# Attention scores from fp16 parts: two full products a head against one full and one 64-row product

## The chip, the cores and the metric

The kernel runs on one core of one Trainium2 chip. The metric is the device time of one execution in microseconds, lower is better; before the change it is 3462.16 us, the median of three runs (3456.29 to 3462.77). TensorE multiplies, VectorE, ScalarE and GpSimd (POOL) work elementwise, SyncE (SP) issues most of the transfers.

## What is computed

Two transformer-like blocks run on a sequence of 2048 positions and width 1024, in float32. The change lies in the attention of the second block: four heads of difference attention (two softmaxes each, the second subtracted) and four heads of stick-breaking attention, all with 64 channels a product. Cut to that:

```python
def diff_attention(q, k, v, lam, lam_init, g):        # q, k: (B,S,H,2,64), v: (B,S,H,128)
    s = einsum('bqhrd,bkhrd->bhrqk', qb, kb) * 64 ** -0.5     # per block of 128 queries, causal prefix
    p = softmax(where(mask, s, -inf))
    attn = p[:, :, 0] - lam * p[:, :, 1]
    o = einsum('bhqk,bkhe->bqhe', attn, vb)           # then a headwise RMSNorm

def stick_breaking_attention(q, k, v, g):             # q, k, v: (B,S,H,64)
    z = einsum('bqhd,bkhd->bhqk', qb, kb) * 64 ** -0.5
    log_1mb = where(mask, log_sigmoid(-z), 0)
    suffix = cumsum(log_1mb, reverse=True) - log_1mb
    a = where(mask, exp(log_sigmoid(z) + suffix), 0)
    o = einsum('bhqk,bkhd->bqhd', a, vb)              # then a headwise RMSNorm
```

TensorE is fed fp16. To keep float32 accuracy every operand x is split into a high part (x rounded to fp16) and a low part (what is left, in fp16), and products of the parts are summed in PSUM.

## The kernel before

`block1` is the first block (about 0 to 950 us of the profile), `block2` the attention of the second (about 960 to 1970), then come `out2` and the feed-forward part `ffn`, which no line of the change touches.

`block2` works through six units, in the order stick, diff, diff, stick, diff, diff. A unit has two heads, r = 0 and 1, of 64 channels each: two heads of stick-breaking attention, or the two softmaxes of one difference head. Each unit first gets its q, k and v by projections, `unit_gemm`: for each of four blocks b of 512 positions, `gemm(b)` runs three projections (`gemm_ct`, lines 142 to 144: 24 products of 512 columns each, into a PSUM bank of the pool `pg`, which has two) for k, v and q, and evacuates each: ScalarE writes the high part, VectorE the low part. v goes by transposing transfers to its tile. For k and q, transfers on SP's queue put the parts where the score products want them.

Where they are wanted: k's tile of a head holds its high part on partitions 0 to 63 and its low part on 64 to 127. q's tile holds, for a head, the high part twice (on both halves of the partitions) and the low part twice. One product of 128 rows thus gives high q times (high k + low k), a second low q times (high k + low k). These are lines 831 and 832 of `scores`; a third product on line 834 adds the mask where the stretch of keys reaches the diagonal. A stretch has up to 512 keys; each score tile takes one PSUM bank of the pool `sc`, which has four.

The tiles of k, v and q come from the pool `up` (U), whose slots are 4 KB a partition: k0, k1, two v, four q, 8 a unit, out of UN = 11.

A row is a block of 128 queries, i = 0 to 15, with W = (i + 1) x 128 keys. In `diff`, head 0's score tiles are evacuated by VectorE (line 894, with a running minimum), then ScalarE takes its exponentials (line 899, pieces of up to 1024 keys), then head 1's the same way; line 914 combines both heads. In `stick`, for each head, all score tiles of the row are made; then, piece by piece of 1024 keys from the last to the first, ScalarE takes sigmoids (972), VectorE scans (974) and GpSimd takes differences (980); line 967 is a GpSimd memset that starts a scan. Both then split the weights into high and low parts (`parts`, lines 844 and 845), turn them by a transposing transfer on SP (847), and multiply them with v (`spread`, lines 868 and 869). The pieces lie in tiles of the pool E, of which there are EN = 10.

The order of each engine's instructions is fixed when the program is built, by a planner that follows the program on a clock of its own: an engine takes the earliest instruction of the program whose operands and buffers are ready. So the projections of the next unit, which stand later in the program, are spread into the gaps of the current one. A tile gets its slot when the first instruction that writes it is placed.

Of the kernel before, what the change touches and what calls it, by code (L numbers as in the profile page):

```python
# [7 lines left out]
F32 = mybir.dt.float32  # L8
# [9 lines left out]
S = 2048  # L18
# [23 lines left out]
UN = 11  # L42
# [24 lines left out]
class Kernel:  # L67
# [713 lines left out]
    def unit_gemm(self, cols):  # L781


        nc = self.nc
        wk, wq, wv = [self.weight(self.a["w2"][cols[c]]) for c in (1, 0, 2)]
        ks = [self.up.tile([128, S], F16, tag="u", name=f"k{r}") for r in range(2)]
        vs = [self.up.tile([128, NT // 2, 2, 128], F16, tag="u", name="v") for _ in range(2)]
        qs = []

        def gemm(b):  # L790
            bs = slice(b * 512, (b + 1) * 512)
            ps = self.gemm_ct(wk, b)
            kh = self.one.tile([128, 512], F16, tag="kh", name="kh")
            kl = self.one.tile([128, 512], F16, tag="kl", name="kl")
            nc.scalar.copy(kh, ps)
            nc.vector.tensor_tensor(kl, ps, kh, ALU.subtract)
            for r in range(2):
                rs = slice(r * 64, (r + 1) * 64)
                nc.sync.dma_start(ks[r][0:64, bs], kh[rs])
                nc.sync.dma_start(ks[r][64:128, bs], kl[rs])  # L800
            ps = self.gemm_ct(wv, b)
            vt = self.one.tile([128, 2, 512], F16, tag="vt", name="vt")
            nc.scalar.copy(vt[:, 0], ps)
            nc.vector.tensor_tensor(vt[:, 1], ps, vt[:, 0], ALU.subtract)
# [12 lines left out]
        return (qs, ks, vs), gemm  # L817

    def scores(self, ops, r, i, strict):

        nc = self.nc
        qs, ks, _ = ops
        q = qs[i // 4][:, r, :, i % 4 * 128:(i % 4 + 1) * 128]
        W = (i + 1) * 128
        out = []
        for p in range(0, W, 512):
            n = min(512, W - p)
            ps = self.score_tile()
            kk = ks[r][:, p:p + n]
            last = p + n == W  # L830
            nc.tensor.matmul(ps[:, 0:n], q[:, 0], kk, start=True, stop=False)  # L831
            nc.tensor.matmul(ps[:, 0:n], q[:, 1], kk, start=False, stop=not last)  # L832
            if last:
                nc.tensor.matmul(
                    ps[:, n - 128:n], self.bias16[:, 2], self.bias16[:, int(strict)], start=False, stop=True
                )
            out.append((ps, p, n))
        return out
# [40 lines left out]
    def diff(self, ops, k, b):  # L879
# [3 lines left out]
        for c in range(4):  # L883
# [66 lines left out]
    def stick(self, ops, k, b):  # L950
# [5 lines left out]
        for c in range(4):  # L956
# [3 lines left out]
            for r in range(2):  # L960
                sc = self.scores(ops, r, i, True)
                pieces, carry = [], None
                for p0 in reversed(range(0, W, PIECE)):
                    n = min(PIECE, W - p0)
                    g, A = self.etiles(n)
                    if carry is None:
                        nc.gpsimd.memset(g[:, n:n + 1], 1.0)  # L967
                    else:
                        nc.vector.tensor_copy(g[:, n:n + 1], carry)
                    for ps, p, w in sc:  # L970
                        if p0 <= p < p0 + PIECE:
                            nc.scalar.activation(g[:, p - p0:p - p0 + w], ps[:, 0:w], AF.Sigmoid, scale=-1.0)
# [4 lines left out]
                    if p0:  # L977
                        carry = self.sm.tile([128, 1], F32, tag="carry", name="carry")
                        nc.vector.tensor_copy(carry, g[:, 0:1])
                    nc.gpsimd.tensor_tensor(A[:, 0:n], g[:, 1:n + 1], g[:, 0:n], ALU.subtract)  # L980
                    pieces.append((self.parts(A, g, n, nc.vector), p0 // 128, n // 128))
                self.spread(pieces, ops, slice(r * 64, (r + 1) * 64), po[:, :, r * 64:(r + 1) * 64])
# [358 lines left out]
```

## Time and profile before

| | before |
|---|---|
| median of three runs | 3462.16 us (3456.29 to 3462.77) |
| the profiled execution | 3461.33 us, span of its instructions 3459.5 us |
| TensorE busy | 3128.8 us, 90% |
| VectorE busy | 2270.6 us, 66% |
| GpSimd busy | 1337.9 us, 39% |
| ScalarE busy | 1217.1 us, 35% |
| granted TensorE clock, mean | 0.958 |

All times within the profile are in microseconds from the first instruction. Matmuls are pipelined: the duration shown for one is longer than the time until the next can start, so prices of products are read from the distance of their starts. PE is TensorE, PEld its weight loads, DVE VectorE, ACT ScalarE, SPq SyncE's queue of transfers.

### The profile page before, as it was taken

To read this page: it belongs to the slowest core of one execution; us is meant where nothing else is said; L and a number is where in the kernel's file an instruction comes from. 1 tells how busy PE (TensorE), PEld (TensorE's weight loads), DVE (VectorE), ACT (ScalarE), POOL (GpSimd) and SP (SyncE) were. 2 spreads that over 40 slices of the span, in tenths; PEclk is the share of its full clock that TensorE was granted. 3 is DMA by queue.
4 is the path that set the end of the run, shared out by engine and by line. 5 is a ranking of instruction groups with operands and counts; after the bars stand their busy time and mean duration, and the time that the engine had idled before them with its cause. 6 is when DMAs were issued, how large, how long until landed. Compare 5 with 4: busy or idle time off the path is not lost. (4 is left out here: it accounts for less than half of the span.)

```text
span 3459.5 us, 46900 instructions
## 1 busy us (share of the span) xinstructions
PE 3128.8 (90%) x17736; PEld 1586.8 (46%) x17736; DVE 2270.6 (66%) x3661; ACT 1217.1 (35%) x2259; POOL 1337.9 (39%) x1181
## 2 busy tenths in 40 slices
PE   8999998999987799868789698999999999789998
PEld 4454454784444455434444343344444444334443
DVE  6986878525648888889785644555655656454436
ACT  5223232322234466644565522332322332221103
POOL 5344354404335544474553400333322232074325
PEclk9999999999998999989999798999999999899999
DMA  5101011216756666546545677422222222533334
GB/s 186 37 17 46 13 50 50 63 32 193 182 139 120 126 124 139 117 102 126 123 100 112 141 176 198 115 67 80 79 83 67 81 83 80 209 129 133 112 109 161
DMA packets 575106, 371.84 MB, mean 107 GB/s; under 512 B 434848, under 2 KB 524704, under 8 KB 573856
## 3 DMA queue, kind: packets, MB, share of 16 engines
q1 hardware_dynamic: 567360, 348.22, 38.9%
q10 hardware_dynamic: 7520, 20.63, 1.7%
q8 instruction: 139, 2.28, 0.3%
q14 instruction: 87, 0.71, 0.1%
HBM read 162.70 MB, written 82.31 MB: 71 GB/s over the span
## 5 line engine op out<-in xcount | busy, mean ns | idle before, releaser
L142 PE MATMUL pg<-th,w 128*128 128x512 f16 x1344 | 522.4, 389 | 39.3 <-DVE r L590 11.8
L144 PE MATMUL pg<-th,w 128*128 128x512 f16 x1344 | 522.2, 389 | 5.9 <-POOL w L155 3.0
L143 PE MATMUL pg<-tl,w 128*128 128x512 f16 x1344 | 522.6, 389 | 0.7 <-DVE tl L181 0.7
L868 PE MATMUL po<-v,e 128*128 128x128 f16 (+1 forms) x1088 | 170.6, 260 | 107.9 <-DMA e<-e 91.2
L980 POOL TENSOR_TENSOR e<-e 128x128 f32<-128x128 f32 (+7 forms) x96 | 165.1, 1723 | 193.7 <-DVE e L974 154.6
L845 POOL TENSOR_TENSOR e<-e 128x1024 f16<-128x1024 f32 (+4 forms) x96 | 154.8, 1627 | 196.5 <-ACT e L844 165.3
L844 ACT CAST e<-e 128x1024 f16<-128x1024 f32 (+7 forms) x192 | 150.4, 794 | 222.8 <-POOL e L967 98.0
L143 PEld LDWEIGHTS <-w 128*128 128x128 f16 x1344 | 134.4, 100 | 182.9 <-issue 46.3
L142 PEld LDWEIGHTS <-w 128*128 128x128 f16 x1344 | 134.5, 100 | 171.0 <-issue 17.5
L144 PEld LDWEIGHTS <-w 128*128 128x128 f16 x1344 | 134.1, 100 | 166.4 <-issue 15.5
L974 DVE TENSOR_TENSOR_SCAN e<-e,few 128x129 f32<-128x129 f32 (+7 forms) x96 | 185.4, 1936 | 34.7 <-POOL e L967 31.4
L1070 POOL TENSOR_TENSOR w<-ws,w 128x1024 f16<-128x1024 f32 x20 | 48.0, 2400 | 393.3 <-ACT w L1069 393.3
L831 PE MATMUL sc<-k,q 128*128 128x512 f16 (+2 forms) x480 | 173.8, 364 | 28.1 <-DVE e L894 22.2
L465 DVE SCALAR_TENSOR_TENSOR acc<-h,cols,acc 128x512 f32<-128x512 f32 x240 | 193.5, 826 | 2.4
L1103 PEld LDWEIGHTS <-w 128*128 128x128 f16 x1232 | 120.7, 98 | 161.6 <-issue 20.5
L1102 PEld LDWEIGHTS <-w 128*128 128x128 f16 x1232 | 120.7, 98 | 150.7 <-ACT w L1069 4.8
L1104 PEld LDWEIGHTS <-w 128*128 128x128 f16 x1232 | 120.7, 98 | 149.6 <-DVE w L1070 4.0
L899 ACT ACTIVATE e<-e,nm 128x1024 f32<-128x1024 f32 (+4 forms) x192 | 171.2, 893 | 51.0 <-DVE e L894 25.8
L832 PE MATMUL sc<-k,q 128*128 128x512 f16 (+2 forms) x480 | 172.2, 366 | 0.0
L868 PEld LDWEIGHTS <-e 128*128 128x128 f16 x1088 | 107.9, 104 | 136.9 <-issue 59.4
L869 PE MATMUL po<-v,e 128*128 128x64 f16 (+1 forms) x1088 | 163.8, 216 | 0.0
L121 POOL TENSOR_TENSOR w<-ws,w 128x1024 f16<-128x1024 f32 x52 | 117.9, 2270 | 113.3 <-ACT w L120 113.2
(317 smaller groups left out, 8000.2 us busy)
## 6 DMA issues: line engine op xcount, KB each, us to landing
mid<-md SPq DMA_DIRECT2D x88, 448.0 KB, 4.2
ws<-in_w SPq DMA_DIRECT2D x48, 512.0 KB, 3.8
md<-mid SPq DMA_DIRECT2D x44, 512.0 KB, 3.4
md<-mid SPq DMA_DIRECT2D x22, 768.0 KB, 5.7
q<-qn SPq DMA_DIRECT2D x96, 128.0 KB, 2.4
ws<-in_wg SPq DMA_DIRECT2D x22, 512.0 KB, 3.5
ws<-in_wu SPq DMA_DIRECT2D x22, 512.0 KB, 4.1
ws<-in_wd SPq DMA_DIRECT2D x22, 512.0 KB, 3.8
```

The source lines that it names most:

```text
L142: nc.tensor.matmul(ps, wh[:, k], th[:, k], start=k == 0, stop=False)
L143: nc.tensor.matmul(ps, wh[:, k], tl[:, k], start=False, stop=False)
L144: nc.tensor.matmul(ps, wl[:, k], th[:, k], start=False, stop=k == KD - 1)
L465: nc.vector.scalar_tensor_tensor(acc[:, ct], src, wcol, acc[:, ct], ALU.mult, ALU.add)
L831: nc.tensor.matmul(ps[:, 0:n], q[:, 0], kk, start=True, stop=False)
L832: nc.tensor.matmul(ps[:, 0:n], q[:, 1], kk, start=False, stop=not last)
L845: eng.tensor_tensor(fv[:, n:2 * n], A[:, 0:n], fv[:, 0:n], ALU.subtract)
L868: nc.tensor.matmul(po, t[:, 0, j], v, start=x == 0, stop=False)
L869: nc.tensor.matmul(po[:, 0], t[:, 1, j], v[:, 0], start=False, stop=x == len(todo) - 1)
L899: nc.scalar.activation(e[r][:, 0:n], e[r][:, 0:n], AF.Exp, bias=nm[:, len(sc) - 1:len(sc)], scale=-1.0, accum_out=ss[:, r, x:x + 1])
L974: nc.vector.tensor_tensor_scan(rev, rev, self.zero.to_broadcast([128, n + 1]), 1.0, ALU.mult, ALU.add)
L980: nc.gpsimd.tensor_tensor(A[:, 0:n], g[:, 1:n + 1], g[:, 0:n], ALU.subtract)
```

## The change

k's high part is doubled: both halves of a head's k tile now hold it, and the low part of both heads goes straight into a third k tile, `kl`, in its natural place (head 0 on partitions 0 to 63, head 1 on 64 to 127). q's tile holds, for each head, the high part on partitions 0 to 63 and the low part on 64 to 127, and a third plane with the high part of both heads in its natural place, which ScalarE writes directly. A score tile is now one product of 128 rows, (high q, low q) times (high k, high k), and one of 64 rows, high q times low k. Low q times low k is no longer computed. `scores` makes the tiles of both heads of a stretch together: two full products, then the two 64-row products, which lie on different halves of the rows. For that, `diff` evacuates the two heads' tiles in turn and takes the exponentials of both afterwards, and `stick` goes through the pieces in the outer loop and the heads in the inner one. A unit takes 9 tiles of U instead of 8, and UN becomes 12.

```diff
-UN = 11
+UN = 12
@@ unit_gemm
-        ks = [self.up.tile([128, S], F16, tag="u", name=f"k{r}") for r in range(2)]
+        ks = [self.up.tile([128, S], F16, tag="u", name=n) for n in ("k0", "k1", "kl")]
...
-            kl = self.one.tile([128, 512], F16, tag="kl", name="kl")
             nc.scalar.copy(kh, ps)
-            nc.vector.tensor_tensor(kl, ps, kh, ALU.subtract)
+            nc.vector.tensor_tensor(ks[2][:, bs], ps, kh, ALU.subtract)
             for r in range(2):
-                rs = slice(r * 64, (r + 1) * 64)
-                nc.sync.dma_start(ks[r][0:64, bs], kh[rs])
-                nc.sync.dma_start(ks[r][64:128, bs], kl[rs])
+                for o in (0, 64):
+                    nc.sync.dma_start(ks[r][o:o + 64, bs], kh[r * 64:(r + 1) * 64])
...
-            qq = self.up.tile([128, 2, 2, 512], F16, tag="u", name="q")
-            qn = self.one.tile([128, 2, 512], F16, tag="qn", name="qn")
-            nc.scalar.activation(qn[:, 0], ps, AF.Copy, scale=0.125)
-            nc.vector.scalar_tensor_tensor(qn[:, 1], ps, 0.125, qn[:, 0], ALU.mult, ALU.subtract)
+            qq = self.up.tile([128, 3, 512], F16, tag="u", name="q")
+            ql = self.one.tile([128, 512], F16, tag="ql", name="ql")
+            nc.scalar.activation(qq[:, 2], ps, AF.Copy, scale=0.125)
+            nc.vector.scalar_tensor_tensor(ql, ps, 0.125, qq[:, 2], ALU.mult, ALU.subtract)
             for r in range(2):
-                for o in (0, 64):
-                    nc.sync.dma_start(qq[o:o + 64, r], qn[r * 64:(r + 1) * 64])
+                rs = slice(r * 64, (r + 1) * 64)
+                nc.sync.dma_start(qq[0:64, r], qq[rs, 2])
+                nc.sync.dma_start(qq[64:128, r], ql[rs])
@@ scores
-    def scores(self, ops, r, i, strict):
+    def scores(self, ops, i, strict, p0=0, end=S):
...
-            ps = self.score_tile()
-            kk = ks[r][:, p:p + n]
-            nc.tensor.matmul(ps[:, 0:n], q[:, 0], kk, start=True, stop=False)
-            nc.tensor.matmul(ps[:, 0:n], q[:, 1], kk, start=False, stop=not last)
+            pss = [self.score_tile() for _ in range(2)]
+            for r, ps in enumerate(pss):
+                nc.tensor.matmul(ps[:, 0:n], q[:, r], ks[r][:, p:p + n], start=True, stop=False)
+            for r, ps in enumerate(pss):
+                rs = slice(r * 64, (r + 1) * 64)
+                nc.tensor.matmul(ps[:, 0:n], q[rs, 2], ks[2][rs, p:p + n], start=False, stop=not last)
@@ diff
-            for r in range(2):
-                sc = self.scores(ops, r, i, False)
-                nm = self.sm.tile([128, 4], F32, tag="nm", name="nm")
-                for x, (ps, p, n) in enumerate(sc):
-                    o = p % PIECE
+            nms = [self.sm.tile([128, 4], F32, tag="nm", name="nm") for _ in range(2)]
+            sc = self.scores(ops, i, False)
+            for x, (pss, p, n) in enumerate(sc):
+                o = p % PIECE
+                for r, (ps, nm) in enumerate(zip(pss, nms)):
                     nc.vector.tensor_scalar(
...
+            for r, nm in enumerate(nms):
                 for x, (e, n) in enumerate(E):
                     nc.scalar.activation(
@@ stick
-            for r in range(2):
-                sc = self.scores(ops, r, i, True)
-                pieces, carry = [], None
-                for p0 in reversed(range(0, W, PIECE)):
-                    n = min(PIECE, W - p0)
+            pieces, carry = [[], []], [None, None]
+            for p0 in reversed(range(0, W, PIECE)):
+                n = min(PIECE, W - p0)
+                sc = self.scores(ops, i, True, p0, p0 + n)
+                for r in range(2):
                     g, A = self.etiles(n)
...
-                self.spread(pieces, ops, slice(r * 64, (r + 1) * 64), po[:, :, r * 64:(r + 1) * 64])
+            for r in range(2):
+                cols = slice(r * 64, (r + 1) * 64)
+                self.spread(pieces[r], ops, cols, po[:, :, cols])
```

## Rows read from the trace of the kernel before

**Rows 1.** The page's part 1: busy time, share of the span, instructions.
```profile
PE 3128.8 (90%) x17736; PEld 1586.8 (46%) x17736; DVE 2270.6 (66%) x3661; ACT 1217.1 (35%) x2259; POOL 1337.9 (39%) x1181
```

**Rows 2.** One window a unit: busy PE, PEld, DVE, ACT, POOL; clock; DMA.
```profile
1020.00:1208.00 188.00, 151.32 (x1043) 79.66 (x1042) 162.64 (x152) 87.14 (x188) 102.08 (x80) 0.90 0.63 125
1215.00:1340.00 125.00, 115.08 (x779) 64.99 (x777) 103.94 (x267) 83.15 (x191) 54.40 (x39) 1.00 0.62 124
1340.00:1455.00 115.00, 108.92 (x719) 62.63 (x717) 96.06 (x262) 80.67 (x183) 51.89 (x40) 1.00 0.67 136
1455.00:1670.00 215.00, 150.79 (x1043) 81.40 (x1040) 192.32 (x184) 101.23 (x216) 126.11 (x110) 0.86 0.57 112
1690.00:1815.00 125.00, 103.97 (x592) 55.81 (x591) 103.08 (x266) 80.10 (x185) 69.82 (x60) 0.92 0.47 102
1838.00:1960.00 122.00, 98.99 (x594) 55.12 (x592) 93.83 (x262) 81.04 (x173) 53.59 (x37) 0.92 0.53 110
```

**Rows 3.** Groups by line and form, TensorE, 994 to 1960 us: busy us, mean ns.
```profile
L831 PE MATMUL sc<-k,q 128*128 128x512 f16 x336 | 133.8, 398 | 23.0 <-DVE e L894 19.9 <-ACT e L972 2.0
...
L831 PE MATMUL sc<-k,q 128*128 128x384 f16 x48 | 16.5, 344 | 3.8 <-ACT e L972 2.2 <-DVE e L894 1.3
```

**Rows 4.** Timeline, TensorE, at 1398.7 us: start, duration, instruction.
```profile
1398.75 0.38 PE L831 MATMUL sc<-k,q 128*128 128x512 f16 x1
1398.96 0.38 PE L832 MATMUL sc<-k,q 128*128 128x512 f16 x1
1399.18 0.38 PE L831 MATMUL sc<-k,q 128*128 128x512 f16 x1
```

**Rows 5.** Timeline, TensorE, 54.8 to 56 us: full products around sixteen of 64 columns.
```profile
54.80 0.38 PE L142 MATMUL pg<-th,w 128*128 128x512 f16 x1
55.11 0.88 PE L352 MATMUL lv<-Q,k 128*64 128x96 f32 x16
55.92 0.39 PE L143 MATMUL pg<-tl,w 128*128 128x512 f16 x1
```

**Rows 6.** Timeline, TensorE, at 1251.5 us: four full f32 products and the next.
```profile
1251.47 0.60 PE L876 MATMUL pt<-ident,o 128*128 128x128 f32 x4
1251.91 0.27 PE L868 MATMUL po<-v,e 128*128 128x256 f16 x1
```

**Rows 7.** Timeline, weight loads, 54.7 to 56.2 us.
```profile
55.11 0.69 PEld L352 LDWEIGHTS lv<-Q,k 128*64 128x64 f32 x16 [0.42 <-issue]
```

**Rows 8.** Timeline, TensorE, 1404.5 to 1407.3 us.
```profile
1404.74 0.38 PE L831 MATMUL sc<-k,q 128*128 128x512 f16 x1
...
1405.17 0.38 PE L143 MATMUL pg<-tl,w 128*128 128x512 f16 x1
1405.39 0.38 PE L831 MATMUL sc<-k,q 128*128 128x512 f16 x1
```

**Rows 9.** Timeline of ScalarE, SP and TensorE: q's evacuation, its transfers, row 11's end.
```profile
1129.46 0.60 ACT L810 ACTIVATE qn<-pg 128x512 f16<-128x512 f32 x1 [0.69 <-PE pg L144]
...
1200.60 1.74 SPq L814 DMA_DIRECT2D q<-qn  x2
...
1126.76 0.22 PE L834 MATMUL sc<-bias 128*128 128x128 bf16 x1
```

**Rows 10.** Timeline, ScalarE, 1949 to 1952 us: exponentials of the last row's head 1.
```profile
1949.56 1.15 ACT L899 ACTIVATE e<-e,nm 128x1024 f32<-128x1024 f32 x1
...
1951.74 0.19 ACT L899 ACTIVATION_READ_ACCUMULATOR e<-e,nm 128x1 f32 x1
```

**Rows 11.** Waits of VectorE, 1030 to 1208 and 1480 to 1670: us, times, longest.
```profile
DVE e L974 <- POOL e L967: 16.8, 12, 1.8
...
DVE e L974 <- POOL e L967: 11.4, 9, 1.8
```

**Rows 12.** DMA issues: instruction, count, KB each, median us to landing.
```profile
q<-qn SPq DMA_DIRECT2D x96, 128.0 KB, 2.4
k<-kh SPq DMA_DIRECT2D x48, 64.0 KB, 2.0
```

More of the change, by code (lines that the diff above doesn't have):

```diff
@@ L821, in scores @@
         nc = self.nc
-        qs, ks, _ = ops
-        q = qs[i // 4][:, r, :, i % 4 * 128:(i % 4 + 1) * 128]
+        qs, ks = ops[:2]
+        q = qs[i // 4][:, :, i % 4 * 128:(i % 4 + 1) * 128]
         W = (i + 1) * 128
         out = []
-        for p in range(0, W, 512):
+        for p in range(p0, min(W, end), 512):
             n = min(512, W - p)
-            ps = self.score_tile()
-            kk = ks[r][:, p:p + n]
             last = p + n == W
-            nc.tensor.matmul(ps[:, 0:n], q[:, 0], kk, start=True, stop=False)
-            nc.tensor.matmul(ps[:, 0:n], q[:, 1], kk, start=False, stop=not last)
-            if last:
[L834 to L837, printed above, removed]
+            pss = [self.score_tile() for _ in range(2)]
[4 more added lines that the diff above has]
+                nc.tensor.matmul(ps[:, 0:n], q[rs, 2], ks[2][rs, p:p + n], start=False, stop=not last)
+            if last:
+                for ps in pss:
+                    nc.tensor.matmul(
+                        ps[:, n - 128:n], self.bias16[:, 2], self.bias16[:, int(strict)], start=False, stop=True
+                    )
+            out.append((pss, p, n))
@@ L959, in stick @@
             W = (i + 1) * 128
-            for r in range(2):
-                sc = self.scores(ops, r, i, True)
-                pieces, carry = [], None
-                for p0 in reversed(range(0, W, PIECE)):
-                    n = min(PIECE, W - p0)
+            pieces, carry = [[], []], [None, None]
[3 more added lines that the diff above has]
+                for r in range(2):
                     g, A = self.etiles(n)
-                    if carry is None:
+                    if carry[r] is None:
                         nc.gpsimd.memset(g[:, n:n + 1], 1.0)
                     else:
[L969 to L972, printed above, removed]
+                        nc.vector.tensor_copy(g[:, n:n + 1], carry[r])
+                    for pss, p, w in sc:
+                        nc.scalar.activation(g[:, p - p0:p - p0 + w], pss[r][:, 0:w], AF.Sigmoid, scale=-1.0)
                     rev = g[:, 0:n + 1][:, ::-1]
@@ L977, in stick @@
                     if p0:
-                        carry = self.sm.tile([128, 1], F32, tag="carry", name="carry")
-                        nc.vector.tensor_copy(carry, g[:, 0:1])
+                        carry[r] = self.sm.tile([128, 1], F32, tag="carry", name="carry")
+                        nc.vector.tensor_copy(carry[r], g[:, 0:1])
                     nc.gpsimd.tensor_tensor(A[:, 0:n], g[:, 1:n + 1], g[:, 0:n], ALU.subtract)
-                    pieces.append((self.parts(A, g, n, nc.vector), p0 // 128, n // 128))
-                self.spread(pieces, ops, slice(r * 64, (r + 1) * 64), po[:, :, r * 64:(r + 1) * 64])
+                    pieces[r].append((self.parts(A, g, n, nc.vector), p0 // 128, n // 128))
+            for r in range(2):
+                cols = slice(r * 64, (r + 1) * 64)
+                self.spread(pieces[r], ops, cols, po[:, :, cols])
             nc.vector.tensor_copy(o8[:, c], po)
```

## The prediction

> **What bounds the kernel now.** I read the page's busy shares first [rows 1]: TensorE 90%, VectorE 66%. Averaged over the kernel that says TensorE, but the change touches only the attention part, 994 to 1960 us, so I cut that into its six units with the windows view [rows 2]. A unit is one call of unit_gemm with its 16 rows of queries; the order is stick, diff, diff, stick, diff, diff. The reader is to see two kinds. In the first stick unit (1020 to 1208) TensorE is busy 151.3 of 188 us and VectorE 162.6; in the second (1455 to 1670) 150.8 against 192.3 of 215. There VectorE sets the pace and TensorE has 37 and 64 us to spare. In diff units two and three (1215 to 1340, 1340 to 1455) TensorE has only 9.9 and 6.1 us left at a clock of 1.00, because the projections of the next unit fill every gap. Units five and six have 21 and 23 us left. So TensorE time is worth something in two units of six, 240 us, and little elsewhere.
>
> **Part 1: the score products, TensorE.** Now each score tile (one head, up to 512 keys) takes two full products, lines 831 and 832. Line 831 has 336 tiles of 512 columns and 48 each of 384, 256 and 128; line 832 as many [rows 3]. Matmul durations overlap (0.38 us shown), so the price is the distance of starts: 0.216 us for 512 columns [rows 4], and in proportion for fewer. Per unit there are 40 groups (row, stretch of keys), each of two heads: 28 groups of 512 columns, 4 each of 384, 256 and 128. A 512 group costs 4 x 0.216 = 0.863 us. After, it is two full products and two of 64 rows, which are to run together: three streams if they do.
>
> Do they? Nothing in the trace uses 64 rows, but the first block uses 64 columns (line 352), the nearest row. Sixteen f32 products of 96 columns go from 55.11 to 55.92, 0.81 us [rows 5]. An f32 product of 128 full columns takes 0.11 us (four in 0.44) [rows 6], so 96 take 0.082 and sixteen in series would need 1.31. So neighbours in different strips do run together.
>
> But the same rows price the change of shape. The last full product starts at 54.80 and the first strip product at 55.11: 0.31 instead of 0.216, and the weight load of the strip starts only then, after 0.42 us of idle load port [rows 5, 7], where between two full products the load is done beforehand. That is 0.094 us; the same 0.31 stands 37 times at full clock. Back again: eight pairs at 0.082 fill 0.66 of the 0.81 us up to the next full product, which leaves at most 0.15 for the way back; I take it to cost what the way in costs. So a round trip costs 0.19 us. For rows instead of columns I bound it by 0 (the load prefetched as between full products) and 0.19, and take 0.19, since the strip is the nearest row and the array is divided in both cases.
>
> The Trainium skill, TensorEngine Tiling (Array Packing), section Key Properties, says that a change of tiling mode, not merely of tile, drains the TensorE. The trace agrees for column strips with the 0.094 us above; by that rule the sum is the one that follows, and without it the first rival's.
>
> Side by side, then, a 512 group costs 3 x 0.216 + 0.19 = 0.84, a gain of only 0.02; a 384 group goes from 0.65 to 0.68, 256 from 0.43 to 0.52, 128 from 0.22 to 0.36. A unit: -28 x 0.02 + 4 x (0.03 + 0.09 + 0.14) = +0.5 us. The saving is eaten by the switches.
>
> It is worse when the pair is torn. Both heads need a score bank. The planner takes the earliest ready product of the program; if only one bank is free, head 0's full product is followed by its own 64-row one, and head 1 comes later: four streams and four switches, +0.38 us per group, 15 us a unit if all. How often? At 1404.7 to 1405.6 score tiles stand singly, with a projection between them [rows 8]; in the two full units 41 of 160 tiles have other work on both sides. I take 30% torn: 0.7 x 0.5 + 0.3 x 15.2 = 4.9 us a unit. In units two and three that is 9.8 us against 16 us of idle TensorE; I charge half, **+5**. In the other four units I charge nothing: 21 to 64 us of idle covers 5; without that cover it would be 20 us. Their clock (0.86 to 0.92, a mix of the levels 1.2 and 2.4 GHz [rows 2]) may move; with room there I don't price it.
>
> **Part 2: the slots of the U pool.** A unit now holds 8 tiles of 11, after it 9 of 12, so three stay free for the next unit either way. Those three are now k0, k1 and the first v; they become k0, k1 and kl, so v and q need slots that this unit gives back: the first v after row 3, the first q after row 7, the second after row 11, everything else after row 15. Before, each came one step sooner. That this wait is real: the third q was ready at 1129.46 and its transfer was issued at 1200.60; row 11 ended at 1126.76 [rows 9]. Moreover q's high part is now written by ScalarE straight into the U tile (no qn in between), so the projection bank (two of them) stays taken until the slot is free; the second v's transposes wait likewise on SP, and vt has one buffer. Behind a waiting evacuation on ScalarE stand exponentials, sigmoids and casts; behind the transposes on SP those of line 847. At the end of unit one I expect the next unit's last q and the k and v of the unit after (done before now) to be missing: 3 blocks x 24 x 0.216 = 15.5 us of TensorE work moved from a unit with room into unit two. Bounds: 0 (it slides on into the second stick unit, which has 64 us) and 15.5. With 11 us of idle left there I charge the excess, **+4**.
>
> **Part 3: both heads interleaved.** In diff, the exponentials of head 0 used to run beside head 1's evacuations; now both follow the last evacuation. Inside the units other rows cover it. At the end nothing does: the last row's head 1 takes from 1949.56 to 1951.93 on ScalarE [rows 10], and head 0's two now stand ahead of it: **+2.4**. If that cover is gone at the end of each of the four diff units, 9.6 us.
> In stick, hi and lo pieces of the two heads alternate and the values wait for both; score banks are filled just before use. VectorE is what counts there: its scans waited 16.8 and 11.4 us behind POOL's line 967 [rows 11]. Two independent chains may fill some of that; more E tiles held until the values' products may add as much. I take 0, with -14 (half of the 28 gone) and +11 (the smaller wait once more) as ends.
>
> **Part 4: transfers.** k: 96 transfers of 64 KB stay, all from kh. q: 96 of 128 KB become 96 of 64 KB; they land in 2.4 us [rows 12] and nobody on the chain waits for them. kl needs no transfer. Evacuations keep number and size. All 0: each unit issues as many as before and q's have half the bytes. What hides them is the previous unit's rows; without these, one landing a unit, 14 us, which is there before and after.
>
> **Sum.** 5 + 4 + 2.4 = +11.4 us on the profiled execution's 3461.3 (span 3459.5 and 1.8 around it): 3472.7. The median shown is 0.8 higher: **3473 us**.
>
> **The rivals.**
> *Faster: the switch costs nothing for rows.* Against it the strip rows [rows 5, 7]; for it that rows are not columns. A unit then saves one stream per group: (28 x 512 + 4 x 768) columns, 7.3 us, 70% of it untorn, 5 us; in the two full units -10. With -14 from the scans and +2.4 at the end, 3440. Either piece alone passes the threshold of 0.2%, 7 us, about what a measurement of this kernel can tell from no change. It decides from a switch under about 0.05 us a way. The Trainium skill, TensorE: Matmul & The Clock Gate, section Measured speedup vs the span model, gives packed products the duration of one plus some 4 ns a tile and names no price for entering; no row here shows that for 64 rows.
> *No change: VectorE hides it all.* In units two and three VectorE is busy 83%, and the projections there are only filler that can slide. Then only the tail counts, 3461 to 3468.
> *Much slower: all pairs torn, or the 64-row products run one after the other.* Torn, 30 us in the two full units, plus 15.5 moved, less 16 idle, plus 2.4: 3494; with the stick's +11, 3505. In series but next to each other, a 512 group costs 4 x 0.216 + 0.19, 0.19 over before, 7.6 us a unit, half of the torn price. It decides from how many score banks come free singly.
>
> **How the numbers follow.** Forecast (3468 to 3483) 0.33; much slower 0.14; no change 0.26; faster 0.27. So faster 0.27, within 0.2% 0.26, slower 0.47. The range goes from the faster case, 3438 with the last 2 us of the tail hidden, to the much slower one, 3505; about 2 in 10 lie outside. The likeliest case's own range is 3468 to 3483.
>
> **What would show it.** In the profile after: the two 64-row starts some 0.01 us apart, and 0.31 from the last full start to the first 64-row start; 0.216 there would show the first rival. The share of torn pairs is countable in the timeline. Units two and three (now 125 and 115 us) should grow by some 4 us each, the stick units stay at 188 and 215. If the third q's transfer isn't later than row 15, part 2 is wrong. Stick units shorter by over 7 us would make the prediction wrong however the products come out.

## The result, and the profile after

The changed kernel takes 3489.9 us (median) against 3462.5 us for the kernel before, measured beside it on the same chip: a ratio of 1.0079, 95% interval 1.0059 to 1.0098. It is slower by 27 us (the interval says 20 to 34), where 11 were forecast. One of the four runs of the changed kernel took 9271 us at a granted clock of 0.352 and is left out of the ratio; the other three took 3484.8 to 3491.9, with a median of 3487.8, 25 us above the kernel before. The profiled execution took 3491.9 us, the longest of these three, and its span is 3490.0. Below, a difference in us is always that of two medians taken side by side: each kernel's against the kernel before that ran next to it. For the changed kernel that is the 27, and 25 by the median of three stands beside it where it matters.

The page's span and busy shares of after, and its two groups of score products (line 832 is the full product, line 835 the 64-row one):

```profile
span 3490.0 us, 46815 instructions
PE 3196.5 (92%) x17736; PEld 1565.2 (45%) x17736; DVE 2271.7 (65%) x3661; ACT 1216.8 (35%) x2259; POOL 1358.1 (39%) x1181
L832 PE MATMUL sc<-k,q 128*128 128x512 f16 (+3 forms) x480 | 166.6, 370 | 28.1 <-DVE e L898 15.0
L835 PE MATMUL sc<-kl,q 64*128 64x512 f16 (+3 forms) x480 | 154.9, 375 | 0.0
```

Against [rows 1] VectorE and ScalarE stand where they were and POOL is busy 20 us longer; TensorE has the same 17736 instructions and is busy 67.7 us longer. A change meant to save a stream of columns per pair of tiles added TensorE time.

Windows of after, one a unit, from the last score product of one unit's row 15 to that of the next (columns as in [rows 2], but cut at other times, so that lengths are to be read from the cuts given in the text):

```profile
1013.00:1202.00 189.00, 155.56 (x985) 73.61 (x984) 154.75 (x145) 82.76 (x182) 98.49 (x77) 0.88 0.57 112
1202.00:1340.00 138.00, 130.01 (x789) 62.10 (x788) 108.30 (x268) 85.53 (x195) 57.01 (x41) 0.92 0.57 109
1340.00:1475.00 135.00, 134.01 (x805) 65.51 (x805) 109.39 (x272) 86.40 (x191) 60.60 (x43) 1.00 0.55 114
1475.00:1681.00 206.00, 162.37 (x1026) 76.65 (x1024) 179.49 (x177) 100.05 (x213) 128.41 (x107) 0.87 0.55 114
1681.00:1837.00 156.00, 135.31 (x766) 63.31 (x766) 128.97 (x285) 91.87 (x202) 90.33 (x68) 0.91 0.52 109
1837.00:1980.00 143.00, 127.42 (x706) 61.21 (x704) 96.27 (x268) 82.71 (x184) 51.74 (x37) 0.94 0.43 91
```

In the third unit TensorE is now busy 134.0 of 135.0 us at a clock of 1.00: it has no gap left in that unit. Cut the same way, before and after, the units ended at these times (us; the last mask product of row 15, line 834 before and 838 after):

| unit | kind | end before | end after | length before | length after |
|---|---|---|---|---|---|
| 1 | stick | 1208.4 | 1202.0 | – | – |
| 2 | diff | 1339.5 | 1340.1 | 131.1 | 138.1 |
| 3 | diff | 1454.7 | 1475.1 | 115.2 | 135.0 |
| 4 | stick | 1668.0 | 1681.4 | 213.3 | 206.3 |
| 5 | diff | 1813.9 | 1836.8 | 145.9 | 155.4 |
| 6 | diff | 1943.4 | 1976.5 | 129.5 | 139.7 |

The first stick unit ends 6.4 us earlier, though its first score product comes 3.0 us later (997.4 against 994.4); the second is 7.0 us shorter. Every diff unit is longer, by 7, 20, 9.5 and 10.

Now the products themselves. Timeline of after, TensorE, around 1397 us: two groups of 512 columns whose 64-row products stand side by side (start, duration, instruction):

```profile
1397.12 0.59 PE L832 MATMUL sc<-k,q 128*128 128x512 f16 x2
1397.65 0.39 PE L835 MATMUL sc<-kl,q 64*128 64x512 f16 x2
1397.97 0.60 PE L832 MATMUL sc<-k,q 128*128 128x512 f16 x2
1398.51 0.39 PE L835 MATMUL sc<-kl,q 64*128 64x512 f16 x2
1398.83 0.39 PE L142 MATMUL pg<-th,w 128*128 128x512 f16 x1
```

Two 64-row products take 0.39 us together, as long as one; their starts lie 3 ns apart. A whole group takes 0.85 us (1397.12 to 1397.97, and 0.86 to 1398.83), where four full products took 0.863 [rows 4]. The pair is real, and it gains nothing: the stream that it saves goes into the two changes of shape.

The same view at 1416.5 us, a torn pair, of which only head 0's tile is there yet, and the weight loads of that stretch (the second fence):

```profile
1416.49 0.38 PE L144 MATMUL pg<-th,w 128*128 128x512 f16 x1
1416.70 0.38 PE L832 MATMUL sc<-k,q 128*128 128x512 f16 x1
1417.02 0.39 PE L835 MATMUL sc<-kl,q 64*128 64x512 f16 x1
1417.33 0.39 PE L142 MATMUL pg<-th,w 128*128 128x512 f16 x1
1417.56 0.38 PE L143 MATMUL pg<-tl,w 128*128 128x512 f16 x1
```

```profile
1417.01 0.09 PEld L835 LDWEIGHTS <-q 64*128 64x128 f16 x1 [0.42 <-issue]
1417.33 0.10 PEld L142 LDWEIGHTS <-w 128*128 128x128 f16 x1 [0.23 <-issue]
1417.35 0.10 PEld L143 LDWEIGHTS <-w 128*128 128x128 f16 x1
```

Alone, a 64-row product costs 0.63 us from the full start to the next full start (1416.70 to 1417.33) where two full products took 0.43. Both changes of shape are seen: 0.32 from full to 64 rows, 0.31 back, instead of 0.216. And the weight loads at either change come only as the new shape starts, as at the column strips [rows 7], while line 143's, between two full products, starts 0.2 us ahead of its product.

Over the attention part, at full clock, the distance of starts from a full product of 512 columns to its 64-row product is 0.312 us in the median (some 250 such distances), and from the 64-row product to the next full one 0.319: 0.096 and 0.103 over 0.216, some 0.20 for a round trip. Counted over all 480 64-row products: **71 of the 240 pairs stand side by side, 409 round trips are made**. That is 70% torn, not 30. 409 x 0.199 = 81 us, less 71 saved streams (43 of 512 columns, 7 of 384, 11 of 256 and 10 of 128, together 12 us), gives 69, and the page has 67.7.

The gated evacuations are seen too. Timeline of after, ScalarE, q's evacuations for the second unit (blocks two and three), and TensorE's last row-15 product of the first unit (third line):

```profile
1136.20 0.59 ACT L809 ACTIVATE q<-pg 128x512 f16<-128x512 f32 x1
1213.54 0.60 ACT L809 ACTIVATE q<-pg 128x512 f16<-128x512 f32 x1
```

```profile
1201.99 0.29 PE L838 MATMUL sc<-bias 128*128 128x128 bf16 x1
```

The third q came at 1129.46 before [rows 9] and comes at 1213.54 now, after row 15; the second at 1136.2, after row 11 (1121.2), where it was 1096.0.

### The profile page after: what moved, and what is told of

It is laid out like the page before. It is cut to its first block, busy times and chain, and to the rows that moved or that the text cites. A ratio compares the mean times of both kernels' runs of the same rounds, so it can differ in the third digit from the quotient of the medians.

```text
span 3490.0 us, 46815 instructions
## 1 busy us (share of the span) xinstructions
PE 3196.5 (92%) x17736; PEld 1565.2 (45%) x17736; DVE 2271.7 (65%) x3661; ACT 1216.8 (35%) x2259; POOL 1358.1 (39%) x1181
## 4 chain that ended last, share of the span: by engine, by line
PE 35%; DVE 8%; issue 3%; POOL 3%; DMA 3%; ACT 1%; SPq 0%; POOLq 0%; ACTq 0%; DVEq 0%
PE pb L1108 3%; PE pb L1110 3%; PE pb L1109 3%; PE pa L1110 2%; PE pa L1108 2%; PE pa L1109 2%; PE pc L1108 2%; PE pc L1109 2%; PE pc L1110 2%; PE pq L665 1%; PE pq L663 1%; PE pq L664 1%; PE pb L1197 1%; PE pb L1196 1%; PE pb L1198 1%
## 5 line engine op out<-in xcount | busy, mean ns | idle before, releaser
L984 POOL TENSOR_TENSOR e<-e 128x1024 f32<-128x1024 f32 (+7 forms) x96 | 171.3, 1791 | 183.9 <-DVE e L978 148.4
L978 DVE TENSOR_TENSOR_SCAN e<-e,few 128x1025 f32<-128x1025 f32 (+7 forms) x96 | 194.9, 2043 | 31.6 <-POOL e L972 24.8
L832 PE MATMUL sc<-k,q 128*128 128x512 f16 (+3 forms) x480 | 166.6, 370 | 28.1 <-DVE e L898 15.0
L835 PE MATMUL sc<-kl,q 64*128 64x512 f16 (+3 forms) x480 | 154.9, 375 | 0.0
```

Of the source, the lines that this page charges most:

```text
L832: nc.tensor.matmul(ps[:, 0:n], q[:, r], ks[r][:, p:p + n], start=True, stop=False)
L978: nc.vector.tensor_tensor_scan(rev, rev, self.zero.to_broadcast([128, n + 1]), 1.0, ALU.mult, ALU.add)
```

## The experiments

The theory after the result: the time is lost to the changes of shape, because most pairs are torn; they are torn because the four score banks come free one at a time. The rivals: the loss is in the waits for U slots, in the interleaved loops, or in something else of the new layout.

**The products alone.** Every 64-row product becomes one of 128 rows; layout, loops and slots stay.

```diff
-                rs = slice(r * 64, (r + 1) * 64)
-                nc.tensor.matmul(ps[:, 0:n], q[rs, 2], ks[2][rs, p:p + n], start=False, stop=not last)
+                nc.tensor.matmul(ps[:, 0:n], q[:, 2], ks[2][:, p:p + n], start=False, stop=not last)
```

> The changed kernel with the 64-row product replaced by one of all 128 rows (high q of both heads times low k of both heads): no change of shape, but four streams a group again; the scores are therefore not the reference's. Loops, slots and transfers stay as changed. Torn pairs with their switches (409 round trips of some 0.2 us in the changed kernel's trace, 66 us of TensorE net): TensorE's busy time falls back to about 3130, the time to 3464 to 3474. U's slots: stays at 3485 or more, since the gated evacuations stay. Loop order: stays at 3485 or more.

Measured: 3467.7 us, ratio 1.0023 (1.0013 to 1.0032), +7.5 us. The page's part 1 of this kernel:

```profile
PE 3128.6 (90%) x17736; PEld 1589.0 (46%) x17736; DVE 2265.6 (65%) x3661; ACT 1214.0 (35%) x2259; POOL 1360.2 (39%) x1181
```

TensorE is back at 3128.6 us, that of [rows 1], and 20 of the 27 us are gone (18 of 25 by the median of three). The changes of shape cost 68 us of TensorE and some 20 of time. By units (ends at 1199.6, 1330.4, 1460.2, 1660.4, 1813.8 and 1950.6) the changed kernel is longer by 2.4, 7.3, 5.2, 6.1, 2.0 and 2.9 us: half of the loss lies outside units two and three. The planner makes a new order for each kernel, but that isn't the reason here: up to 1559 us of the full-row kernel (1574 of the changed one) TensorE, VectorE, ScalarE and GpSimd run the same instructions in the same order in both (transfers not counted), and the changed kernel is 15 us behind by then.

**Pairs kept together.** Both heads' score tiles become one tile of two banks, so that they come free at once.

```diff
-            self.sc = self.pool("sc", SCN, PSUM, ctx=c2)
+            self.sc = self.pool("sc", SCN // 2, PSUM, ctx=c2)
...
-            pss = [self.score_tile() for _ in range(2)]
+            pair = self.sc.tile([128, 2, 512], F32, tag="sc", name="sc")
+            pss = [pair[:, 0], pair[:, 1]]
```

> The changed kernel with both heads' score tiles as one tile of two banks (two such tiles instead of four single ones), so that both heads' products always get their banks together and the 64-row products stand side by side. Torn pairs: round trips fall from 409 to about 240, each saving a stream as well; TensorE's busy time falls by 50 to 65 us to about 3135 to 3150, the time to 3462 to 3478. U's slots or loop order: 3485 or more; if the coarser turn of the banks costs something, more than 3490.

Measured: 3485.6 us, ratio 1.0074 (1.0059 to 1.0089), +25.4 us. The page's part 1:

```profile
PE 3134.6 (90%) x17736; PEld 1549.3 (44%) x17736; DVE 2258.2 (65%) x3661; ACT 1215.6 (35%) x2259; POOL 1353.3 (39%) x1181
```

The cause of the tearing is settled: 235 of 240 pairs now stand side by side, with 245 round trips, and TensorE falls by 62 us. Not all of the torn pairs had to wait long for the second bank: in 58 of the 165 groups of the changed kernel in which the 64-row product of head 0 stands ahead of head 1's full one, that full product is the very next on TensorE. An order that waits that little was not tried. The time was expected to fall with it and hardly did. So it needs the same tile without the 64-row products.

> Both edits of the first two experiments: the 64-row product made one of all 128 rows (high q of both heads times low k of both, so the scores are not exactly the reference's), and both heads' score tiles as one tile of two banks. There is no switch of shape left to tear. If the two-bank tile costs time of its own (VectorE and ScalarE get their tiles in coarser turns), the time is 3478 to 3490, about that of the two-bank kernel with 64-row products (3485.6). If it doesn't, and the two-bank kernel was slow for its switches, the time is 3462 to 3472, that of the full-row kernel (3467.7).

```diff
-                nc.tensor.matmul(ps[:, 0:n], q[rs, 2], ks[2][rs, p:p + n], start=False, stop=not last)
+                nc.tensor.matmul(ps[:, 0:n], q[:, 2], ks[2][:, p:p + n], start=False, stop=not last)
```

Measured, with that edit on top of the two-bank tile: 3491.9 us, ratio 1.0087 (1.0071 to 1.0104), +30.6 us; TensorE:

```profile
PE 3132.6 (90%) x17736; PEld 1588.9 (45%) x17736; DVE 2251.6 (64%) x3661; ACT 1216.5 (35%) x2259; POOL 1357.1 (39%) x1181
```

The two-bank tile costs 23 us by itself (30.6 less 7.5). One thing that it does is seen in VectorE's waits in the third unit (us in total, times, longest). With 64-row products, single banks (the changed kernel, 1340 to 1475) first, two-bank tile (1341 to 1479) second:

```profile
DVE sums L912 <- ACT e L904: 8.9, 5, 3.0
DVE sums L913 <- ACT e L905: 18.5, 7, 4.5
```

With full products, single banks (1330 to 1460) first, two-bank tile (1331 to 1480) second:

```profile
DVE sums L911 <- ACT e L903: 10.1, 5, 3.2
DVE sums L912 <- ACT e L904: 12.3, 5, 4.0
```

VectorE's row sums wait longer for ScalarE's exponentials. Over the whole attention part these waits are 20.6 us with single banks and 35.6 with the two-bank tile, and 25.1 and 37.9 with full products; TensorE's score products wait 27.8 and 61.3 us for VectorE and ScalarE to evacuate a bank, and 50.7 and 66.8 with full products. With two tiles of two banks the next scores can start only when both heads of a stretch are evacuated; that these waits make up the 23 us is argued, not shown. The pair of kernels also gives the price of an untorn pair: TensorE 3134.6 against 3132.6, +2.0 us over all 240 groups (the prediction: +0.5 a unit, 3). In time the 64-row products are at -5 us there, with intervals that overlap: no gain that can be told from none.

**All pairs torn.** The other end: head 0's 64-row product right behind its full one.

```diff
             for r, ps in enumerate(pss):
                 nc.tensor.matmul(ps[:, 0:n], q[:, r], ks[r][:, p:p + n], start=True, stop=False)
-            for r, ps in enumerate(pss):
                 rs = slice(r * 64, (r + 1) * 64)
```

> The changed kernel with each head's 64-row product written right behind its full one, so that no two stand side by side. Round trips of shape rise from 409 to 480 and the 71 shared streams are lost: TensorE's busy time rises by 14 + 14 us to about 3225. If TensorE's time is worth what the full-row kernel showed (68 us of it made 22 us), the time is 3494 to 3504. If tearing isn't what costs, it stays at 3485 to 3492.

Measured: 3504.4 us, ratio 1.0126 (1.0111 to 1.0141), +42.1 us; 480 round trips and no pair. TensorE in the timeline at 1401 us and the page's part 1:

```profile
1401.13 0.38 PE L832 MATMUL sc<-k,q 128*128 128x512 f16 x1
1401.44 0.39 PE L834 MATMUL sc<-kl,q 64*128 64x512 f16 x1
1401.76 0.39 PE L832 MATMUL sc<-k,q 128*128 128x512 f16 x1
1402.08 0.39 PE L834 MATMUL sc<-kl,q 64*128 64x512 f16 x1
```

```profile
PE 3225.7 (92%) x17736; PEld 1575.1 (45%) x17736; DVE 2260.7 (65%) x3661; ACT 1217.2 (35%) x2259; POOL 1353.9 (39%) x1181
```

Every start is 0.31 to 0.32 from the last. Against the changed kernel 71 more round trips (71 x 0.199 = 14 us) and 71 more streams (12 us) are 26 us; TensorE is busy 29.2 us longer, and the time is 14.7 us longer (17 by the median of three). The first 68 us of TensorE cost 20, these 29 cost 15. It looks as if the next are the dearer the more of the idle time is used up, but with intervals of 7 us or more either way on both differences that is not shown.

**The loops, without the products.** The kernel before, with its products and its k and q, but in the changed kernel's two loops; then each loop alone. The edit of the stick loop:

```diff
-            for r in range(2):
-                sc = self.scores(ops, r, i, True)
-                pieces, carry = [], None
-                for p0 in reversed(range(0, W, PIECE)):
-                    n = min(PIECE, W - p0)
+            pieces, carry = [[], []], [None, None]
+            for p0 in reversed(range(0, W, PIECE)):
+                n = min(PIECE, W - p0)
+                sc = self.scores2(ops, i, True, p0, p0 + n)
+                for r in range(2):
...
+    def scores2(self, ops, i, strict, p0=0, end=S):
...
+            for r, ps in enumerate(pss):
+                q = qs[i // 4][:, r, :, i % 4 * 128:(i % 4 + 1) * 128]
+                kk = ks[r][:, p:p + n]
+                nc.tensor.matmul(ps[:, 0:n], q[:, 0], kk, start=True, stop=False)
+                nc.tensor.matmul(ps[:, 0:n], q[:, 1], kk, start=False, stop=not last)
```

> The kernel before with the changed loops alone: scores of both heads made together, diff with both evacuations ahead of both exponentials, stick with pieces outside and heads inside; products, U tiles and transfers as before. Torn pairs or U's slots: 3450 to 3467, the stick units some 6 us shorter each, the tail 2 us longer. Loop order as the cause: 3475 to 3490.

Measured, both loops: 3459.7 us, ratio 0.9995 (0.9986 to 1.0005), -0.5 us. Together they cost nothing.

> The kernel before with the changed loop in stick alone (pieces outside, heads inside); diff as before. If interleaving the heads helps the two stick units and hurts the diff units at the end, as the units' ends with both loops say (20 us ahead after the fourth unit, 2 at the end): 3440 to 3453. If the gain with both loops was the plan's luck: 3456 to 3466.

Measured, the stick loop alone: 3445.9 us, ratio 0.9957 (0.9942 to 0.9972), **-15.5 us**. Its windows, first and second stick unit and the diff unit after the second:

```profile
1004.00:1192.00 188.00, 150.75 (x1046) 79.74 (x1045) 152.33 (x147) 84.20 (x184) 101.74 (x78) 0.94 0.60 122
...
1446.00:1645.00 199.00, 142.87 (x985) 78.13 (x983) 171.81 (x172) 92.82 (x205) 121.08 (x103) 0.84 0.54 111
1645.00:1804.00 159.00, 126.07 (x783) 67.87 (x782) 130.03 (x284) 92.75 (x205) 90.61 (x70) 0.92 0.53 112
```

The first stick unit ends at 1192.0 instead of 1208.4, the second takes 199 us instead of 213: 31 us, of which the diff units after them give 20 back. The third has 288 products of the projections instead of 240, work that used to lie in the first unit's gaps. The fifth takes 159 us instead of 146, with fewer products of the projections (208 instead of 221) but 350 products with v instead of 290: part of the second stick unit's work now lies behind its last score. By the last score of all, 11 us are left of the gain; the rest of it, some 6 us, lies behind, where nothing was changed. VectorE's scans wait for POOL less than in [rows 11]; the same view of this kernel in its first stick unit:

```profile
DVE e L994 <- POOL e L988: 11.6, 9, 1.8
```

11.6 us instead of 16.8; in the second (1446 to 1645) 8.4, where the kernel before has 14.6 (1455 to 1668). That is 11 us of shorter waits, at the place that the prediction named. But the scans' waits for ScalarE's sigmoids grow by 6 us in the two units (4.3 and 3.3 instead of 1.5 and none), so the waits make up 5 us of the gain and where the rest comes from is not shown.

```diff
-            for r in range(2):
-                sc = self.scores(ops, r, i, False)
-                nm = self.sm.tile([128, 4], F32, tag="nm", name="nm")
-                for x, (ps, p, n) in enumerate(sc):
-                    o = p % PIECE
+            nms = [self.sm.tile([128, 4], F32, tag="nm", name="nm") for _ in range(2)]
+            sc = self.scores2(ops, i, False)
+            for x, (pss, p, n) in enumerate(sc):
+                o = p % PIECE
+                for r, (ps, nm) in enumerate(zip(pss, nms)):
...
+            for r, nm in enumerate(nms):
```

> The kernel before with the changed loop in diff alone (both heads' evacuations, then both heads' exponentials); stick as before. If the loops' effects add (both 3459.7, stick alone 3445.9, before 3461.3): 3470 to 3480. If the prediction's tail of 2.4 us were all: 3461 to 3467.

Measured, the diff loop alone: 3472.3 us, ratio 1.0029 (1.0018 to 1.0040), **+10.0 us**. Its last score product comes 7.8 us later than before (1951.2 against 1943.4), with units three to six longer by 4.0, 4.2, 3.7 and 3.5 us and unit two shorter by 6.8; the other 3.7 us of its span come behind the last scores. The forecast tail isn't what they are. The last row's exponentials now stand in one run, but ScalarE starts it before the last evacuation ends at 1955.8:

```profile
1953.66 1.15 ACT L921 ACTIVATE e<-e,nm 128x1024 f32<-128x1024 f32 x1 [0.54 <-issue]
1957.07 1.14 ACT L921 ACTIVATE e<-e,nm 128x1024 f32<-128x1024 f32 x1
```

The run ends 2.4 us behind that evacuation and 7.0 behind the last score product; before, the exponentials of [rows 10] ended 2.5 behind the last evacuation, which ends at 1949.3, and 8.4 behind the last score product. What lengthens the units, the fourth of them a stick unit whose loop is the old one, was not isolated. The two loops' effects don't add: -15.5 and +10.0 would be -5.5, and together they are -0.5.

```diff
-UN = 11
+UN = 12
```

> The same with UN = 12 (four U tiles free for the next unit instead of three). If slots matter: 3432 to 3448, some 5 us below the same loop with 11. If not: within 3 us of it.

Measured, with a twelfth slot on top of the stick loop: **3441.2 us**, ratio 0.9942 (0.9928 to 0.9957), -20.1 us: faster than both kernels. Its four runs (3439.7 to 3442.4) all lie below the four of the stick loop alone (3444.4 to 3448.6), by some 5 us as expected if slots matter, but the intervals of the two ratios overlap, and a new plan comes with the slot.

**The slots.** The kernel before with one U slot less; then the changed kernel with one more, for which q's low part and a small scratch tile share memory with other tiles.

```diff
-UN = 11
+UN = 10
```

> The kernel before with UN = 10 instead of 11, nothing else: q and v of the next unit get their slots one step later, as in the changed kernel. U's slots cost what lies between the full-row kernel (3467.7) and the loops alone (3459.7): 3464 to 3474, the loss in the second and third unit. If slots cost nothing and those 8 us come from q's evacuation into the U tile or from the plan: 3456 to 3463.

Measured: 3458.0 us, ratio 0.9990 (0.9981 to 1.0000). With two free slots instead of three for the next unit, the second and third unit share their time otherwise (124 and 125 us instead of 131 and 115), and the sum stays.

```diff
-UN = 12
+UN = 13
...
-            ql = self.one.tile([128, 512], F16, tag="ql", name="ql")
+            ql = self.one.tile([128, 512], F16, tag="qn", name="ql")
...
-        junk = self.one.tile([128, 128], F32, tag="junk", name="junk")
+        junk = self.one.tile([128, 128], F32, tag="m1", name="junk")
```

> The changed kernel with 13 U slots instead of 12 (room made by letting two small scratch tiles share slots of the pool mixer). q's and v's evacuations then come one step sooner, as before the change. Torn pairs: the time falls by 0 to 6 us only (3484 to 3490). U's slots: by 10 to 20 us (3470 to 3480). Loop order: unchanged within 4 us.

Measured: 3500.8 us, ratio 1.0119 (1.0104 to 1.0135), +40.6 us. The waits eased in part: the second unit's second q is evacuated at 1094.9 instead of 1136.2, but the third at 1214.2, as late as in the changed kernel (1213.5). No time came of it: the first four units end 6 us later than in the changed kernel (1687.5 against 1681.4). The fifth then takes 185 us instead of 155. By the program the shared scratch has further users in the fourth and fifth unit (the tiles of lines 1008 and 1014, of a part that runs beside them), so the total of this kernel says nothing on slots. At the end of the third unit it is 6 us late too, which gives no sign that a slot is what lacks; since the third q still waits, it doesn't rule it out.

**What is left of the layout.** Between both loops on the old layout (-0.5 us) and full products on the new one (+7.5) lie 8 us. Two attempts. q's high part goes through a scratch tile and a transfer, so that its evacuation no longer waits for a U slot:

```diff
-            nc.scalar.activation(qq[:, 2], ps, AF.Copy, scale=0.125)
-            nc.vector.scalar_tensor_tensor(ql, ps, 0.125, qq[:, 2], ALU.mult, ALU.subtract)
+            qh = self.one.tile([128, 512], F16, tag="qh", name="qh")
+            nc.scalar.activation(qh, ps, AF.Copy, scale=0.125)
+            nc.vector.scalar_tensor_tensor(ql, ps, 0.125, qh, ALU.mult, ALU.subtract)
+            nc.sync.dma_start(qq[:, 2], qh)
...
-                nc.sync.dma_start(qq[0:64, r], qq[rs, 2])
+                nc.sync.dma_start(qq[0:64, r], qh[rs])
```

> The changed kernel with q's high part evacuated into a scratch tile and sent from there to its U tile, so that ScalarE and the projection bank don't wait for the U slot. If that wait is what lies between the full-row kernel and the loops alone (8 us): 3480 to 3486. If not: 3487 to 3494.

Measured: 3487.2 us, ratio 1.0076 (1.0061 to 1.0091), +24.9 us: 2.5 less than the changed kernel, with overlapping intervals, though its third q comes at 1146.6 instead of 1213.5. And the full products in the old order, each head's two next to each other, on the edit of the full rows:

```diff
             for r, ps in enumerate(pss):
                 nc.tensor.matmul(ps[:, 0:n], q[:, r], ks[r][:, p:p + n], start=True, stop=False)
-            for r, ps in enumerate(pss):
                 nc.tensor.matmul(ps[:, 0:n], q[:, 2], ks[2][:, p:p + n], start=False, stop=not last)
```

> The full-row kernel of the first experiment (the 64-row product made one of all 128 rows of both heads, so the scores are not exactly the reference's) with each head's two products next to each other, as in the kernel with the loops alone, instead of both heads' first products and then both second ones. It differs from the loops alone (3459.7) then only in the layout of q and k, the U tiles and the evacuations. If the order of the four products is what costs those 8 us: 3457 to 3463. If layout, slots or evacuations: 3465 to 3471.

Measured: 3471.4 us, ratio 1.0036 (1.0024 to 1.0049), +11.7 us. The order of the products isn't the cause. The third unit's window, first of both loops on the old layout, second of the full-row kernel on the new one:

```profile
1328.00:1444.00 116.00, 112.95 (x742) 64.45 (x741) 98.08 (x266) 79.52 (x183) 54.45 (x38) 1.00 0.65 128
```

```profile
1330.00:1460.00 130.00, 125.27 (x807) 70.97 (x806) 109.09 (x276) 87.01 (x194) 62.42 (x41) 1.00 0.57 120
```

65 more matmuls and 12 us more of TensorE lie in it, work moved there from elsewhere, as part 2 of the prediction had it for the second unit; later units give some back. But the last kernel, with the same layout, loses its time elsewhere: its third unit takes 118.3 us, against 116.0 with both loops on the old layout, and units one, two and five take 5, 5 and 9.5 us more and the sixth 10 less. So where the 8 us lie goes with the plan. Neither slots on the old layout nor the freed evacuation moved the total, and the cause of the 8 us stays open.

## Why the prediction was right or wrong

The sign was right and 3489.9 lies in the range, 17 us above the forecast, outside the likeliest case's own 3468 to 3483 and near the much slower rival (3494). It is in the range only because the range was drawn out to that rival; the sum itself was less than half of what was measured, and two of its steps were wrong.

**The price of a change of shape: right.** 0.094 us each way was taken from column strips; for rows it is 0.096 in and 0.103 back. The choice of the strip as the nearest row, against the bound of 0, held, and with it the first rival fell. The Trainium skill, TensorEngine Tiling (Array Packing), section Key Properties, says that a change of mode drains the TensorE; the trace agrees, by these two numbers and by the weight load that starts with the new shape. The Trainium skill, TensorE: Matmul & The Clock Gate, section Measured speedup vs the span model, gives packed products the time of one and about 4 ns for each further tile; the trace agrees inside a pair (3 ns). What that section does not name, the way into and out of the pair, is where the gain went.

**Side by side no gain: right.** 0.85 us a group of 512 columns (0.84 forecast), +2.0 us over all groups with untorn pairs (3 forecast).

**The torn share: the step that failed.** 30% was taken from how single score tiles stood in the kernel before [rows 8]; it was 70% (169 of 240). The tiles counted as single there showed neighbours of another kind on both sides; what counts now is that both banks be free when head 0's full product starts, which is rarer, as the two-bank tile shows. With 70% the prediction's own formula gives 0.3 x 0.5 + 0.7 x 15.2 = 10.8 us a unit, 65 in all, and 67.7 was measured (62.5 of it in the attention part, up to the last score).

**Where it counts: the second step that failed.** Only units two and three were charged, by half; with the right share that would still be 11 us. The runs show 20, half of it in the four units held to be covered by 21 to 64 us of idle TensorE (cut at its last score, the sixth had 15, not 23). The likely reason is that a window's idle time is no cover for a product that a row of scores waits for: it is an average over moments at which the engine is free and others at which it isn't. Which products were waited for was not traced. The clock explains little of it: in the six units (the first from 1000 us on) it is 0.88, 0.92, 1.00, 0.87, 0.91 and 0.94 after and 0.90, 0.93, 1.00, 0.88, 0.92 and 0.91 with full rows.

**Part 2: the wait right, the place wrong, the price not shown.** The third q did come after row 15. But the moved blocks, expected in unit two, went to unit three: 264 products of the projections instead of 288 in the second, 312 instead of 240 in the third. And slots cost nothing on the kernel before (-3.4 us with one less, at the edge of its interval) and gave nothing on the changed one. The charge of 4 stands beside an unexplained 8.

**Part 3: both sizes off, in opposite directions.** Tail +2.4: in the changed kernel the last exponential ends at 1981.65, 3.8 us behind the last evacuation where it was 2.5, so 1.3 of the 2.4 came at that place; from the last score product on, it is even 3.3 us sooner (5.1 instead of 8.4). The diff loop costs 10.0 all the same, but inside units three to six, one of them a stick unit: that this is close to the bound of 9.6, named for the cover gone at the end of each diff unit, is luck. Stick 0: the loop gains 15.5, near the bound of -14. Together -0.5 instead of +2.4. The stick units' shortening, which the prediction had named as its refutation above 7 us, came at that threshold: 6.4 us by the first one's end (9.4 from its first score product on) and 7.0 for the second. It was paid back by diff.

**The sum by steps:** 5 became 20, 4 became 8 (cause open, and 12 with the other order of the full products), 2.4 became -0.5: 27 instead of 11.

## What to carry to other kernels

At the prices measured here, products on parts of the array pay only if several streams are saved for each change of shape; one stream of 512 columns (0.216 us) is about what one round trip (0.199) costs, and a pair that a scarce bank tears apart costs a round trip for each half and saves nothing. When several edits come together, price and run each alone: here a stick loop worth 15 us and a diff loop costing 10 lay hidden in a change that lost 27, and the stick loop alone is the version to keep (3446 us, 3441 with a twelfth slot). Idle time in a window need not be cover for work that stands in the window's own chain.

## What was not expected of the hardware

The change of shape costs the same whatever the width: from a full product of 512, 384, 256 and 128 columns to the 64-row product of the same width the starts lie 0.312, 0.259, 0.205 and 0.152 us apart, 0.096 to 0.098 over 0.216 and, in proportion, 0.162, 0.108 and 0.054; back it is 0.319, 0.266, 0.212 and 0.159, 0.103 to 0.105 over (medians of 30 or more each at full clock). At 128 columns each way thus costs nearly twice the stream itself. And it is nearly the same for halves of the rows as for strips of 64 columns (0.094, [rows 5]).
